# A hybrid attention block in Strassen-Winograd pairs: gate functions moved into the first products, two loads moved a pair ahead, buffers shared out anew

## The chip, the cores and the metric

The kernel runs on one core of a Trainium2 chip. The core has a matrix engine (TensorE, PE; its weight loads are shown as PEld), a vector engine (VectorE, DVE), a scalar engine for functions (ScalarE, ACT), a general engine (GpSimd, POOL) and an engine that issues most of the transfers (SyncE, SP). Each works through its own queue in order. The metric is the device time of one launch in microseconds; lower is better.

## The reference

One layer of a decoder block on x of 1024 positions by 1024 channels, all in fp32. The input is normalised, one projection gives all parts, two token mixers run beside each other (retention, differential attention), each is normalised per head and multiplied by SiLU of its gate, projected, multiplied by a sigmoid gate, and the sum goes through the output projection.

```python
h = rms_norm(x, norm_g)
z = einsum('bsd,dn->bsn', h, w_in)
(q_r, k_r, v_r, gate_r, q_d, k_d, v_d, gate_d, mg_r, mg_d) = split(z, ...)
o_r = rms_norm(retention(q_r, k_r, v_r), ret_norm_g) * silu(gate_r)
y_r = einsum('bse,ed->bsd', o_r, ret_w_o)
o_d = rms_norm(diff_attention(rms_norm(q_d), rms_norm(k_d), v_d, lam), sub_g) * 0.8
o_d = o_d * silu(gate_d)
y_d = einsum('bse,ed->bsd', o_d, diff_w_o)
m = sigmoid(mg_r) * y_r + sigmoid(mg_d) * y_d
x = x + einsum('bsd,de->bse', m, w_out)
```

## The kernel before

Each fp32 operand is split into a high and a low part, and a product is three matmuls (high x high, high x low, low x high; lines 101 and 126 to 133). The program runs in these stages.

1. The input is normalised and transposed; projections and retention follow, then eight heads of the differential attention. Work that is due later is handed to a clock (`after`, `tick`, `drain`) and mixed among the matmuls of the next products (`among`).
2. The gates: four projections of 1024 columns (two for SiLU, two for sigmoid), cut into 16 pairs of 2 x 128 columns: q = 0 to 7 are SiLU pairs, 8 to 15 sigmoid pairs. Each pair is one Strassen-Winograd step of 2 x 2 blocks with seven products. Two of the seven are made early, in `first_duo`, where both pairs of a duo use the two PSUM banks of the tag `pj`: the first half (kh 0) gives the product P1, the second (kh 1) adds P2 to it, which is the finished block C11. Both are copied out of PSUM (line 232 on ACT, line 234 on DVE) through tiles `ft` of the tag `gt` (three buffers) and stored to `first_d` in DRAM. Duos 0 and 2 run at the end of retention, 4 to 10 at the end of the attention, with its last heads still in the mix, and 12 and 14 after that.
3. The gate stage, `rests(pairs)`: for each pair the five products that are left, in `one` and `two` of the class `Pair`. A pair's `first` loads P1 (`p1_h`, shown as `p_h` in the profile) and copies it into the bank `y` (line 899), to which products are added; ACT copies `y` out between them (`u2`, `u3`, line 843: `u_h`), and the next product must wait for that copy. DVE subtracts `u` from the bank `z` (`c_h`, line 837), ACT applies the function (lines 914, 918), in the SiLU pairs DVE multiplies by the mixer's output `o` (line 915), and SP stores the result to `og` or `sg`. One pair ahead, `prep` loads the pair's weights (`ra_h`, `rb_h`), makes their sums and splits (`s_h`, `ls_h`, `l_h`), and then (line 925 on) loads C11 back into `c_first`, applies the function on ACT, multiplies and stores it.
4. The two projections of the mixers (`y0`, `y1`: first products, then pairs again, with gates `s` and sums `m` loaded as `ld` tiles), and the output projection (`out`) with x loaded as `ld` tiles.

Right operands of the gate stage: `t_h` are sums of quarters of the transposed input, loaded on POOL's queue and split on ACT and DVE (lines 690, 691); `hT` are the quarters that are still there.

Buffers of the later stages, each 128 x 512 fp32: results `c` come from the tag `gt` (three), `p1` has two, `u2` and `u3` two each, and `ld` (o, s, m, x) four. Those but `gt` lie in a pool that is opened when the attention's pool is closed. Instructions are put in order within each engine's queue when the program is built, and buffers turn round in a ring: an instruction that writes into a buffer waits for the last use of what was in it.

Of the kernel before, what the change touches and what calls it, by code (L numbers as in the profile page):

```python
# [9 lines left out]
F32 = mybir.dt.float32  # L10
# [52 lines left out]
def tile_hybrid_block(ctx, tc, x, norm_g, w_in, ret_norm_g, ret_w_o, dq_g, dk_g,  # L63
# [160 lines left out]
    def first_duo(q, following):  # L224

        banks = [pst("pj", f"fb{q + i}") for i in range(2)]
        for kh in range(2):
            among(sum([product(banks[i], F[q + i][kh], hq[kh, 0], kh == 0) for i in range(2)], []))
            for i in range(2):
                t = gp.tile([P, 512], F32, tag="gt", name=f"ft{q + i}{kh}", bufs=3)  # L230
                if kh == 0:
                    nc.scalar.activation(t, banks[i], AF.Copy)  # L232
                else:
                    nc.vector.tensor_copy(t, banks[i])
                nc.sync.dma_start(first_d[q + i][:, kh, :], t)
            if kh == 0:
                following()
            tick()
# [585 lines left out]
    class Pair:  # L824
# [15 lines left out]
        def u(self, tag):  # L840

            t = temp(tag, f"{tag}_{self.name}", 2)
            nc.scalar.activation(t, self.y, AF.Copy)  # L843
            return t
# [47 lines left out]
    def gate_pair(q):  # L892
        br, gate = q // 4 % 2, q < 8

        def first():
            p1 = temp("p1", f"p1_h{q}", 2)
            nc.sync.dma_start(p1, first_d[q][:, 0, :])
            y = bank(f"y_h{q}", "g")
            nc.scalar.activation(y, p1, AF.Copy)
            return y  # L900

        def pre(strip, half):
            if gate:
                h = 2 * (q % 4) + strip
                o = temp("ld", f"o{br}{h}{half}", 4)
# [3 lines left out]
        def done(strip, half, src, t, o):  # L909
# [3 lines left out]
            if gate:  # L913
                nc.scalar.activation(t, src, AF.Silu)
# [9 lines left out]
        def prep_and_c11():  # L924
            prep()
            t = temp("c", f"c_first{q}")
            nc.sync.dma_start(t, first_d[q][:, 1, :])
            done(0, 0, t, t, pre(0, 0))
# [27 lines left out]
    for br, wo in enumerate((ret_w_o, diff_w_o)):  # L956
        def calls(p, br=br):
            whole_sum = br == 1 and p == 3

            def pre(strip, half):  # L960
                i = 2 * p + strip
                o = [temp("ld", f"s{br}{i}{half}", 4)]
                nc.sync.dma_start(o[0], rows(sg[br][i], half))
                if whole_sum:
                    o.append(temp("ld", f"m{i}{half}", 4))
# [33 lines left out]
    def calls_out(i):  # L999
# [4 lines left out]
        def pre(strip, half):  # L1004
            xt = temp("ld", f"xr{i}{strip}{half}", 4)
# [40 lines left out]
```

## Time and profile before

| | us |
|---|---|
| median of 3 runs (1316.33 to 1317.63) | 1316.62 |
| the profiled execution, whole | 1319.1 |
| its span | 1317.3 |
| TensorE busy | 1263.8 |
| granted clock, mean | 0.991 |

All times in the text are microseconds from the start of the profiled span. A row of the timeline has start, length, engine, line, operation, output<-input, count, and in brackets the idle time ahead of it with what ended it. Buffer numbers are left out in the names: `c_h<-z_h,u_h` stands for all pairs. A row of `SPq` or POOL with DMA_DIRECT2D is the issue of a transfer. In the waits, "A <- B" says that A's engine stood idle until B was done.

### The profile page before, as it was taken

To read this page: it belongs to the slowest core of one execution; us is meant where nothing else is said; L and a number is where in the kernel's file an instruction comes from. 1 tells how busy PE (TensorE), PEld (TensorE's weight loads), DVE (VectorE), ACT (ScalarE), POOL (GpSimd) and SP (SyncE) were. 2 spreads that over 40 slices of the span, in tenths; PEclk is the share of its full clock that TensorE was granted. 3 is DMA by queue.
4 is the path that set the end of the run, shared out by engine and by line. 5 is a ranking of instruction groups with operands and counts; after the bars stand their busy time and mean duration, and the time that the engine had idled before them with its cause. 6 is when DMAs were issued, how large, how long until landed. Compare 5 with 4: busy or idle time off the path is not lost.

```text
span 1317.3 us, 19920 instructions
## 1 busy us (share of the span) xinstructions
PE 1263.8 (96%) x6836; PEld 1112.6 (84%) x6836; DVE 903.9 (69%) x1928; ACT 683.6 (52%) x1522; POOL 288.2 (22%) x403
## 2 busy tenths in 40 slices
PE   7998999999999999999999998998889999999798
PEld 5877888889999999999999886887778887877587
DVE  6777534745777868787787854865546688886583
ACT  6233213526676757667676743644554664443440
POOL 3133203323433425343332302000000000014100
PEclk9999999999999999999999999999899999999899
DMA  7375320240120201021020347887655887878873
GB/s 258 97 234 174 96 80 8 79 155 8 42 60 7 65 9 57 10 57 52 15 81 9 112 148 276 281 271 239 205 198 194 260 285 248 290 241 222 242 223 116
DMA packets 165173, 187.78 MB, mean 143 GB/s; under 512 B 10944, under 2 KB 109392, under 8 KB 165072
## 3 DMA queue, kind: packets, MB, share of 16 engines
q1 hardware_dynamic: 159936, 173.12, 40.7%
q0 software_dynamic: 5136, 13.39, 4.1%
q8 instruction: 54, 0.88, 0.3%
q14 instruction: 47, 0.39, 0.1%
HBM read 131.94 MB, written 54.53 MB: 142 GB/s over the span
## 4 chain that ended last, share of the span: by engine, by line
PE 66%; DMA 13%; issue 11%; DVE 5%; ACT 2%; POOL 2%; SPq 1%; DVEq 0%; POOLq 0%; ACTq 0%
PE z_d L121 20%; PE y_h L130 6%; PE fb L130 5%; PE sps L563 5%; PE dops L603 5%; PE z_rqk L121 5%; PE z_rv L121 4%; PE z_h L130 4%; PE y_out L130 2%; PE aT L590 2%; DMA og<-cb 2%; DMA c_first<-first 2%; DMA or_wr<-in_w_out_dram 2%; PE z_out L130 2%; DMA md<-cb 2%
## 5 line engine op out<-in xcount | busy, mean ns | idle before, releaser
L121 PE MATMUL z_d<-w_d,hT 128*128 128x384 f32 x1536 | 300.6, 340 | 0.6 <-DVE nsq L518 0.6
L121 PEld LDWEIGHTS z_d<-w_d,hT 128*128 128x128 f32 x1536 | 264.1, 188 | 2.8 <-DVE nsq L518 0.9
L569 ACT ACTIVATE S<-S,ast 128x256 f32<-128x256 f32 (+7 forms) x128 | 98.7, 772 | 29.3 <-DVE ast L565 27.9
L563 PE MATMUL sps<-K,Q 128*128 128x512 f32 (+5 forms) x384 | 107.8, 364 | 0.3 <-ACT Q L544 0.3
L130 PE MATMUL y_h<-t_h,ls_h 128*128 128x512 f32 x384 | 96.9, 403 | 11.3 <-ACT u_h L843 11.3
L130 PE MATMUL fb<-hT,fw 128*128 128x512 f32 x384 | 96.6, 402 | 7.5 <-ACT ft L232 7.1
L130 PEld LDWEIGHTS y_h<-t_h,ls_h 128*128 128x128 f32 x384 | 73.9, 194 | 29.5 <-ACT u_h L843 14.0
L121 PE MATMUL z_rv<-w_rv,hT 128*128 128x512 f32 x384 | 98.7, 397 | 0.0
L121 PE MATMUL z_rqk<-w_rqk,hT 128*128 128x512 f32 x384 | 95.9, 403 | 1.5 <-ACT hT L284 1.5
L130 PEld LDWEIGHTS fb<-hT,fw 128*128 128x128 f32 x384 | 71.6, 192 | 22.5 <-ACT ft L232 7.8
L121 PEld LDWEIGHTS z_rqk<-w_rqk,hT 128*128 128x128 f32 x384 | 72.0, 193 | 16.5 <-ACT hT L284 2.1
L603 PE MATMUL dops<-V,aTs 128*128 128x128 f32 x576 | 81.7, 275 | 0.0
L603 PEld LDWEIGHTS dops<-V,aTs 128*128 128x128 f32 x576 | 78.5, 191 | 2.6
L980 POOL DMA_DIRECT2D md<-cb x6 | 5.6, 933 | 337.9 <-DVE cb L973 337.9
L121 PEld LDWEIGHTS z_rv<-w_rv,hT 128*128 128x128 f32 x384 | 68.8, 188 | 11.8
L565 DVE CUSTOM_DVE_ANT_0 S<-sps,ndist 128x512 f32<-128x512 f32 (+5 forms) x128 | 67.6, 535 | 5.1 <-PE sps L563 4.6
L91 POOL TENSOR_TENSOR nss<-ms_n,mh 128x4 f32<-128x4 f32 x64 | 65.9, 1029 | 4.1
L520 POOL TENSOR_TENSOR nsq<-nsq,gh 128x256 f32<-128x256 f32 x64 | 50.1, 787 | 73.4 <-DVE nsq L518 61.8
L563 PEld LDWEIGHTS sps<-K,Q 128*128 128x128 f32 x384 | 63.3, 190 | 2.3 <-ACT Q L544 0.9
L580 DVE SCALAR_TENSOR_TENSOR S<-S,ast,S 128x128 f32<-128x128 f32 (+3 forms) x64 | 56.6, 884 | 1.3
L130 PE MATMUL y_y<-t_o,ls_y 128*128 128x512 f32 x192 | 47.9, 393 | 5.1 <-ACT ls_y L690 4.2
L90 POOL TENSOR_SCALAR ms_n<-nss 128x4 f32<-128x4 f32 x64 | 18.2, 285 | 154.6 <-DVE nss L514 151.9
(226 smaller groups left out, 2672.2 us busy)
## 6 DMA issues: line engine op xcount, KB each, us to landing
wr_d<-in_w_in_dram SPq DMA_DIRECT2D x96, 128.0 KB, 2.6
fr<-in_w_in_dram SPq DMA_DIRECT2D x16, 512.0 KB, 4.3
first<-ft SPq DMA_DIRECT2D x32, 256.0 KB, 2.5
ra_h<-in_w_in_dram SPq DMA_DIRECT2D x16, 512.0 KB, 4.2
rb_h<-in_w_in_dram SPq DMA_DIRECT2D x16, 512.0 KB, 4.7
s<-sg SPq DMA_DIRECT2D x32, 256.0 KB, 5.3
xt<-in_x_dram SPq DMA_DIRECT2D x8, 512.0 KB, 7.9
wr_rqk<-in_w_in_dram SPq DMA_DIRECT2D x16, 256.0 KB, 5.7
```

The lines of the kernel that those rows point to most:

```text
L90: nc.gpsimd.tensor_scalar(ms, ss, m, EPS, ALU.mult, ALU.add)
L91: nc.gpsimd.tensor_tensor(out_t, ms, mh[:, :n], ALU.pow)
L121: nc.tensor.matmul(o, a[k][:, i0, asl], b[k][:, i1, bsl], start=(k == 0 and j == 0), stop=(k == NK - 1 and j == 2))
L130: nc.tensor.matmul(bank, L[:, i0, j * P:(j + 1) * P], R[:, j, i1, :], start=(start and j == 0 and i == 0), stop=(j == 3 and i == 2), skip_ ...
L520: nc.gpsimd.tensor_tensor(sq, sq, hd["g"], ALU.mult)
L563: nc.tensor.matmul(sp[:, :m], hd["Q"][t][:, j, e, :], hd["K"][:, j, c], start=(e == 0), stop=(e == 1))
L565: nc.vector.tensor_tensor_reduce(sb[:, c], sp[:, :m], ndist[:, S - n + m * f:S - n + m * f + m], -slope, FMAX if f == 0 else st[:, j:j + 1 ...
L569: nc.scalar.activation(sb[:, :n], sb[:, :n], AF.Exp, bias=st[:, j:j + 1], scale=-1.0, accum_out=st[:, 2 + j:3 + j])
L580: nc.vector.scalar_tensor_tensor(S0[:, :n], S1[:, :n], st[:, 6:7], S0[:, :n], ALU.mult, ALU.add)
L590: nc.tensor.transpose(tp[:, b * P:(b + 1) * P], A[:, c:c + P], ident)
L603: nc.tensor.matmul(o[:, :P], aT[:, b, :], hd["V"][f][:, b, :], start=(kb == 0), stop=(kb == t))
L980: nc.gpsimd.dma_start(m, t, accum_op=ALU.add)
```

## The change

- In `first_duo` both halves are copied out by ACT. The second half gets the gate's function at once: Silu for q below 8, Sigmoid from 8 on. For the sigmoid pairs the finished block goes straight to its place in `sg`, and is not loaded again. Duos 12 and 14 take their tiles from `ld` instead of `gt`.
- In the gate stage P1 is loaded in `prep`, one pair ahead, into an `ld` tile. C11 is loaded in the SiLU pairs alone; it needs no function any more, only the multiply by `o`.
- Result tiles `c`: every fourth comes from a tile of its own, so four for three. `ld` has six buffers for four; `p1` has none of its own, `u3` one for two.

```diff
+    GATE = {0: AF.Silu, 1: AF.Sigmoid}
+
+    def first_duo(q, following, room=None):
...
-                t = gp.tile([P, 512], F32, tag="gt", name=f"ft{q + i}{kh}", bufs=3)
-                if kh == 0:
-                    nc.scalar.activation(t, banks[i], AF.Copy)
-                else:
-                    nc.vector.tensor_copy(t, banks[i])
-                nc.sync.dma_start(first_d[q + i][:, kh, :], t)
+                t = (room(f"ft{q + i}{kh}") if room else
+                     gp.tile([P, 512], F32, tag="gt", name=f"ft{q + i}{kh}", bufs=3))
+                nc.scalar.activation(t, banks[i], GATE[q // 8] if kh else AF.Copy)
+                dst = first_d[q + i][:, kh, :]
+                if kh and q >= 8:
+                    dst = sg[(q - 8) // 4][2 * ((q + i) % 4)][:, 0:512]
+                nc.sync.dma_start(dst, t)
...
     def temp(tag, name, bufs=None):
         if tag == "c":
-            return gp.tile([P, 512], F32, tag="gt", name=name, bufs=3)
+            turn["c"] = turn.get("c", 0) + 1
+            if turn["c"] % 4:
+                return gp.tile([P, 512], F32, tag="gt", name=name, bufs=3)
+            bufs = 1
...
-            t = temp(tag, f"{tag}_{self.name}", 2)
+            t = temp(tag, f"{tag}_{self.name}", 2 if tag == "u2" else 1)
...
+        p1 = []
+
         def first():
-            p1 = temp("p1", f"p1_h{q}", 2)
-            nc.sync.dma_start(p1, first_d[q][:, 0, :])
             y = bank(f"y_h{q}", "g")
-            nc.scalar.activation(y, p1, AF.Copy)
+            nc.scalar.activation(y, p1[0], AF.Copy)
             return y
...
-                o = temp("ld", f"o{br}{h}{half}", 4)
+                o = temp("ld", f"o{br}{h}{half}", 6)
...
             if gate:
-                nc.scalar.activation(t, src, AF.Silu)
+                if src is not None:
+                    nc.scalar.activation(t, src, AF.Silu)
                 nc.vector.tensor_tensor(t, t, o, ALU.mult)
...
         def prep_and_c11():
+            p1.append(temp("ld", f"p1_h{q}", 6))
+            nc.sync.dma_start(p1[0], first_d[q][:, 0, :])
             prep()
-            t = temp("c", f"c_first{q}")
-            nc.sync.dma_start(t, first_d[q][:, 1, :])
-            done(0, 0, t, t, pre(0, 0))
+            if gate:
+                t = temp("c", f"c_first{q}")
+                nc.sync.dma_start(t, first_d[q][:, 1, :])
+                done(0, 0, None, t, pre(0, 0))
...
-    first_duo(12, lambda: more(14, 15))
+    def room(name):
+        return temp("ld", name, 6)
+
+    first_duo(12, lambda: more(14, 15), room)
...
-    first_duo(14, pairs[0].prep)
+    first_duo(14, pairs[0].prep, room)
```

The loads of `s`, `m` and `xr` in the projections ask for six buffers in the same way.

The change also moves instructions in the queues. The names below carry the number of the pair (`c_first6` is C11 of pair 6; `ft121` is the tile of pair 12, second half), and a counter at the end that is without meaning here.

**The last duos, SP's queue**, where the last output of the attention (`ot_d7<-doT71`) is stored. Before:

```order
L235 DMA first11_121<-ft111_9126 128x512
L643 DMA ot_d7_87<-doT71_9108 128x512
L906 DMA o000_9295<-ot_r0_78 128x512
L235 DMA first12_122<-ft120_9165 128x512
L897 DMA p1_h0_9381<-first0_110 128x512
L906 DMA o011_9386<-ot_r0_78 128x512
L906 DMA o020_9429<-ot_r0_78 128x512
L766 DMA rb_h1_9401<-in_w_in_dram 128x4x256
L906 DMA o010_9467<-ot_r0_78 128x512
L897 DMA p1_h1_9471<-first1_111 128x512
L235 DMA first13_123<-ft130_9168 128x512
L765 DMA ra_h2_9490<-in_w_in_dram 128x4x256
```

After, at the same place:

```order
L238 DMA sg04_96<-ft101_9123 128x512
L937 DMA c_first0_9295<-first0_110 128x512
L937 DMA c_first1_9428<-first1_111 128x512
L238 DMA sg06_98<-ft111_9126 128x512
L646 DMA ot_d7_87<-doT71_9108 128x512
L937 DMA c_first2_9517<-first2_112 128x512
L238 DMA first12_122<-ft120_9165 128x512
L238 DMA first13_123<-ft130_9168 128x512
L769 DMA rb_h1_9402<-in_w_in_dram 128x4x256
L238 DMA sg10_100<-ft121_9211 128x512
L768 DMA ra_h2_9490<-in_w_in_dram 128x4x256
L238 DMA sg12_102<-ft131_9214 128x512
```

Four loads of `o` and two of P1 that stood between the stores of duo 12 have moved behind them; three loads of C11 stand ahead instead, two of them ahead of the attention's last store.

**A SiLU pair, ACT's queue** (`c_h…` is the Silu of a result, `l22` a split, `u2` the copy of the bank). Before:

```order
L914 ACTIVATE c_h211_9703<-c_h211_9703 128x512
L914 ACTIVATE c_h101_9708<-c_h101_9708 128x512
L690 ACTIVATE l22_h4_9757<-rb_h4_9737 128x512
L843 ACTIVATE u2_h3_9770<-y_h3_9719 128x512
L914 ACTIVATE c_first4_9763<-c_first4_9763 128x512
L690 ACTIVATE ls4_h4_9760<-s4_h4_9743 128x512
L914 ACTIVATE cb210_9808<-y_h2_9596 128x512
```

After, and below it SP's queue in a SiLU pair of the changed kernel:

```order
L921 ACTIVATE c_h311_9823<-c_h311_9823 128x512
L921 ACTIVATE c_h201_9828<-c_h201_9828 128x512
L693 ACTIVATE l22_h5_9877<-rb_h5_9857 128x512
L849 ACTIVATE u2_h4_9889<-y_h4_9837 128x512
L693 ACTIVATE ls4_h5_9880<-s4_h5_9863 128x512
L921 ACTIVATE cb310_9927<-y_h3_9715 128x512
```

```order
L923 DMA og01_89<-c_h201_9828 128x512
L912 DMA o110_9955<-ot_d1_81 128x512
L769 DMA rb_h7_10101<-in_w_in_dram 128x4x256
L923 DMA og10_90<-c_first5_9883 128x512
L912 DMA o101_9957<-ot_d0_80 128x512
L937 DMA c_first6_10005<-first6_116 128x512
L912 DMA o131_9962<-ot_d3_83 128x512
L923 DMA og01_89<-cb310_9927 128x512
L933 DMA p1_h6_9976<-first6_116 128x512
L768 DMA ra_h8_10222<-in_w_in_dram 128x4x256
L923 DMA og10_90<-c_h411_9945 128x512
```

The activation of C11 is gone from ACT. On SP the load of `c_first6` waits for the store of `c_first5`, two rows ahead of it, since both use the same tile; P1 of pair 6 is loaded in the pair before.

**The end of the attention, ACT's queue** (`S` is the exponential of the scores, `fw` a weight split, `Q`, `aTs` and `fsq` copies and squares of the attention). Before:

```order
L232 ACTIVATE ft50_8716<-fb5_8620 128x512
L84 ACTIVATE fw100_8992<-fr10_8990 128x512
L592 COPY aTs740_8641<-aT740_8636 128x512
L544 ACTIVATE Q77_8708<-tq77_8703 128x2x128
L545 ACTIVATE Q77_8708<-tq77_8703 64x2x128
L546 ACTIVATE Q77_8708<-tq77_8703 64x2x128
L625 ACTIVATE fsq70_8661<-O70_8338 128x512
L569 ACTIVATE S751_8563,ast75_8530<-S751_8563,ast75_8530 128x768
```

After:

```order
L234 ACT_TABLE_LOAD
L234 ACTIVATE ft41_8810<-fb4_8619 128x512
L84 ACTIVATE fw100_8992<-fr10_8990 128x512
L595 COPY aTs740_8641<-aT740_8636 128x512
L547 ACTIVATE Q77_8708<-tq77_8703 128x2x128
L548 ACTIVATE Q77_8708<-tq77_8703 64x2x128
L549 ACTIVATE Q77_8708<-tq77_8703 64x2x128
L628 ACTIVATE fsq70_8661<-O70_8338 128x512
L572 ACT_TABLE_LOAD
L572 ACTIVATE S751_8563,ast75_8530<-S751_8563,ast75_8530 128x768
L234 ACT_TABLE_LOAD
L234 ACTIVATE ft51_8813<-fb5_8620 128x512
```

Each change between exponential and gate function brings a load of the function table: 14 in the whole program, where there were 9 (one at the start, eight in the gate stage).

More of the change, by code (lines that the diff above doesn't have):

```diff
@@ L1004, in pre @@
         def pre(strip, half):
-            xt = temp("ld", f"xr{i}{strip}{half}", 4)
+            xt = temp("ld", f"xr{i}{strip}{half}", 6)
             nc.sync.dma_start(xt, place(x, strip, half))
```

5 lines of the change are left out of this document (2 added, 3 removed).

## The prediction

> **What bounds the kernel now.** I read the page first, then busy times by stretch, then the order of instructions in time where TensorE (PE) is not full.
>
> ```profile
> span 1317.3 us, 19920 instructions
> PE 1263.8 (96%) x6836; PEld 1112.6 (84%) x6836; DVE 903.9 (69%) x1928; ACT 683.6 (52%) x1522; POOL 288.2 (22%) x403
> ```
>
> PE is the bound over the whole span, so only stretches in which it stands still or runs on a lower granted clock can be won. The change removes no matmul. The stretches:
>
> ```profile
> 770.00:830.00 60.00, 53.42 (x249) 44.09 (x248) 30.28 (x51) 23.05 (x42) 11.56 (x19) 0.94 0.66 221
> 880.00:970.00 90.00, 79.26 (x332) 63.41 (x330) 50.16 (x80) 44.27 (x72) 0.00 (x0) 0.96 0.68 220
> 970.00:1062.00 92.00, 91.41 (x396) 75.51 (x397) 57.25 (x89) 53.60 (x98) 0.00 (x0) 0.98 0.70 230
> 1200.00:1260.00 60.00, 51.22 (x214) 40.56 (x213) 35.85 (x58) 23.06 (x41) 13.97 (x21) 0.94 0.89 252
> ```
>
> Columns: stretch, length, busy PE, PEld, DVE, ACT, POOL, granted clock, DMA share, GB/s. PE loses time in the last two first-product duos (770 to 830), in the Silu pairs of the gate stage (880 to 970) and where the output projection begins (1200 to 1260); the sigmoid pairs (970 to 1062) are nearly full. How much the Silu pairs lose, from PE's own rows:
>
> ```profile
> 883.12 2.88 PE L130 MATMUL y_h<-t_h,l_h 128*128 128x512 f32 x12
> ...
> 918.57 3.02 PE L130 MATMUL y_h<-t_h,ls_h 128*128 128x512 f32 x12 [2.66 <-ACT u_h L843]
> ...
> 982.09 2.88 PE L130 MATMUL y_h<-t_h,l_h 128*128 128x512 f32 x12
> ...
> 995.69 2.88 PE L130 MATMUL y_h<-t_h,l_h 128*128 128x512 f32 x12
> ...
> 1036.49 2.88 PE L130 MATMUL y_h<-t_h,l_h 128*128 128x512 f32 x12
> ```
>
> The product with `l_h` comes once in each pair. From 995.69 to 1036.49 lie three pairs: 13.60 each, with no wait. From 883.12 to 982.09 lie six: 98.97, where 6 x 13.60 = 81.6 would do. **The Silu pairs lose 17.4 us**, waits and the slower matmuls behind them together. The reason stands on ACT:
>
> ```profile
> 911.77 0.63 ACT L914 ACTIVATE c_h<-c_h 128x512 f32<-128x512 f32 x1
> ...
> 913.78 0.32 SPq L927 DMA_DIRECT2D c_first<-first  x1
> ...
> 916.88 0.63 ACT L914 ACTIVATE c_first<-c_first 128x512 f32<-128x512 f32 x1 [4.48 <-DMA c_first<-first]
> 917.42 0.61 ACT L690 ACTIVATE l_h<-rb_h 128x512 fp32r<-128x512 f32 x1
> 917.94 0.58 ACT L843 ACTIVATE u_h<-y_h 128x512 f32<-128x512 f32 x1
> ```
>
> ACT stands at the activation of the reloaded C11 (`c_first`) until its load lands; behind it in the queue is `u_h`, the copy that PE needs before it may add to the bank again. PE's row at 918.57 is released by just that copy.
>
> **The change, part by part.**
>
> *Gate stage.* The activation of `c_first` leaves ACT's queue: 16 of them, 0.63 each, 10 us of ACT, and with it the wait. What is then late?
>
> ```profile
> PE y_h L130 <- ACT u_h L843: 7.5, 5, 3.2
> ACT c_first L914 <- DMA c_first<-first: 11.3, 6, 4.5
> DVE c_first L915 <- DMA o<-ot_d: 7.8, 4, 3.3
> ```
>
> (Total, times, longest, from 830 to 970.) DVE still multiplies `c_first` by `o` in the Silu pairs, and the order shows the `o` load of that multiply behind the same store as before. So DVE keeps waits like those of the last row, 1.95 in the mean, 3.3 at most. How much PE bears: without the c_first wait, in the pair whose last Silu begins at 911.77 and ends near 912.4, `l_h` and `u_h` would be done near 913.5, while PE had work up to 918.57 - 2.66 = 915.9; 2.4 of slack. The longest wait exceeds that by 1, the mean doesn't; I charge 0.4 for each of six pairs, 2.4. **Term A: -17.4 + 2.4 = -15.0**, bounds 0 (the wait moves whole) and -17.4. In the sigmoid pairs c_first disappears altogether, with 8 loads, 8 stores and 8 activations; PE waited little there, so I take nothing. `u3` with one buffer is read by DVE a pair before it is written again: nothing.
>
> *Last duos.* The two stalls of the duos at their end:
>
> ```profile
> 797.76 13.87 PE L130 MATMUL fb<-hT,fw 128*128 128x512 f32 x60
> 811.96 3.01 PE L130 MATMUL fb<-hT,fw 128*128 128x512 f32 x12 [0.33 <-DVE ft L234]
> 821.22 7.61 PE L130 MATMUL fb<-hT,fw 128*128 128x512 f32 x24 [6.24 <-ACT ft L232]
> 828.66 1.52 PE L130 MATMUL z_h<-t_h,ls_h 128*128 128x512 f32 x6
> ```
>
> ```profile
> 808.04 0.63 ACT L690 ACTIVATE t_h<-t_h 128x512 fp32r<-128x512 f32 x1 [2.65 <-DMA t_h<-h_t]
> ...
> 809.80 13.74 SPq L235 DMA_DIRECT2D first<-ft  x4
> ...
> 811.85 0.63 ACT L690 ACTIVATE t_h<-t_h 128x512 fp32r<-128x512 f32 x1 [0.37 <-DMA t_h<-h_t]
> ...
> 820.57 0.60 ACT L232 ACTIVATE ft<-fb 128x512 f32<-128x512 f32 x1 [8.08 <-DMA first<-ft]
> ```
>
> ACT waits 8.08 for one of three `gt` tiles to be stored, and PE for ACT. At 13.60/60 = 0.227 a matmul the 96 matmuls from 797.76 would end at 819.5; they end at 828.66: 9.1 lost, part of it to the clock (24 matmuls in 7.61 where 5.4 would do). With six `ld` tiles this wait goes. Next late are the `t_h` conversions that now stand ahead of the copies on ACT, and twelve of them are due before the pairs start: the first four ran at 808.04 to 811.85, 1.27 apart; the twelfth would be at 808.04 + 11 x 1.27 = 822.0, cut and subtracted at 823.3. **Term B: 823.3 - 828.66 = -5.4**, bounds 0 and -9.1.
>
> *Gate functions in the duos.* The copies on DVE (16 x 0.69) become ACT functions. On DVE that is off the path. On ACT they bring switches of the function table:
>
> ```profile
> 952.44 0.62 ACT L690 ACTIVATE ls_h<-s_h 128x512 fp32r<-128x512 f32 x1
> 953.08 1.28 ACT L914 ACT_TABLE_LOAD   x1
> 954.37 0.60 ACT L914 ACTIVATE cb<-y_h 128x512 f32<-128x512 f32 x1
> ```
>
> ```profile
> 745.00:755.00 10.00, 10.00 (x55) 8.61 (x54) 9.47 (x27) 7.49 (x19) 1.38 (x3) 1.00 0.45 149
> 755.00:765.00 10.00, 10.00 (x54) 8.60 (x54) 7.04 (x17) 5.53 (x11) 0.86 (x1) 1.00 0.43 131
> ```
>
> ```profile
> 756.23 0.37 ACT L609 ACTIVATE O<-dops,ast 128x128 f32<-128x128 f32 x1 [3.15 <-PE dops L603]
> ```
>
> A load is 1.28 and from 953.06 (the end before it) to 954.37 pass 1.31. The order has 14 loads for 9; seven of the new ones stand between Exp and Silu or Sigmoid at the end of the attention, with eight moved functions of 0.60: 7 x 1.28 + 8 x 0.60 = 13.8 us of ACT. Where they are densest, 745 to 765, ACT has 13.0 of 20 busy and gets four loads and two functions, 6.3: 19.3 of 20. It just fits. PE's next matmul behind each function has other work ahead of it in PE's order (12 matmuls of the other bank, scores, transposes), so I charge little: **term D: +1**, bounds 0 and +13.8. In the Silu to Sigmoid turn of the gate stage four loads fewer remain; that is in term A.
>
> The Trainium skill speaks against this part: in "ScalarE: Activation LUTs", What ACT_TABLE_LOAD costs, a switch is a load of 1283 ns and a drain of about 1380 ns, and the page's advice is to do all of one set before switching. The rows above show the load, but no drain beyond 0.03 us; by the page's price the seven switches and eight functions would be an estimated 7 x 2.66 + 4.8 = 23.4 of ACT instead of 13.8, and the forecast with all of it on PE's path 1317 instead of 1308. By the rows the trace does not agree with the drain.
>
> *Six load tiles, four result tiles in the projections.* At the start of the output projection:
>
> ```profile
> L130 PE MATMUL X_out<-r_w,la_out 128*128 128x512 f32 x96 | 24.8, 415 | 8.5 <-ACT la_out L690 7.7 <-ACT y_out L819 0.8
> ```
>
> ```profile
> 1229.03 5.09 DMA m<-md
> ```
>
> The load of `m`, a load tile that had to wait for its turn, is on the chain of waits; with six it is issued earlier. But PE's 8.5 us hang on stores to `md` and loads of `rf_out`, which stay. **Term C: -2**, bounds +1 and -8.5.
>
> **Sum:** -15.0 - 5.4 + 1 - 2 = -21.4. The profiled execution took 1319.1 (span 1317.3); the median of the runs is 1316.6. 1316.6 - 21.4 = **1295**.
>
> **Rivals.**
>
> *The wait goes from ACT to DVE.* For it: DVE waits in order as ACT did, and c_first's multiply has the splits and `c_h` of the pair behind it. If its `o` wait falls on PE in full, six pairs keep 6 x 1.95 = 11.7, and term A is -5.7: 1304. Against it: 2.4 of slack in each pair.
>
> *ACT becomes the bound of the attention's end.* For it: 19.3 of 20. If all 13.8 fall on PE: 1295 + 12.8 = 1308. Against it: ACT has gaps there like the 3.15 before 756.23, and PE other work.
>
> *More comes back.* Terms A, B at their bounds and C at -4: 1316.6 - 17.4 - 9.1 + 1 - 4 = 1287.
>
> *Slower: C11's own tile.* With four result tiles in a Silu pair every fourth is the new one, and it is always c_first; the order shows each c_first load behind the store of the c_first before it. That is a ring: multiply, store, load, multiply.
>
> ```profile
> c_first<-first SPq DMA_DIRECT2D x6, 256.0 KB, 3.3
> ...
> og<-c_first SPq DMA_DIRECT2D x3, 256.0 KB, 2.6
> ```
>
> ```profile
> first<-ft SPq DMA_DIRECT2D x9, 256.0 KB, 5.7
> ...
> o<-ot_r SPq DMA_DIRECT2D x4, 256.0 KB, 9.7
> ```
>
> By the first two rows (880 to 970) the ring takes 0.7 + 2.6 + 3.3 and two issues of 0.3: 7.2, under 13.6. By the last two (797 to 830, with the queues full) it takes 0.7 + 5.7 + 9.7 + 0.6 = 16.7, and eight pairs at 16.7 lose 24.8, 7.4 more than now; without terms B and C, which full queues would take too, and with +1, 1325. It decides from a ring of 13.6 + 17.4/8 = 15.8. Against it: the change takes 4 MB of transfers out and the pairs before 880 kept their pace.
>
> *Nothing moves.* The stores, not the tiles, are late, and the waits stay where they are under other names: 1316.6, with term D 1318.
>
> **How the numbers follow.** Forecast 1295 (1290 to 1300) 0.50; wait to DVE 0.18 (1300 to 1308); ACT the bound 0.09 (1302 to 1310); more comes back 0.10 (1284 to 1290); nothing moves 0.06; slower 0.07. The predicted time is that of the likeliest, 1295. The range 1287 to 1310 leaves out half of "more", all of "nothing" and "slower": 0.18. Of a measurement of this kernel 0.2%, 2.6 us, can be told from no change: faster 0.87, same 0.06, slower 0.07.
>
> **What would show it.** Term A: the `l_h` products of the Silu pairs 13.6 to 14.2 apart, and no ACT wait for c_first; if DVE waits over 3 us for c_first or `o` and PE behind it for ACT's `u_h`, the first rival holds, and if c_first's multiply waits for a load issued as its own last store lands, the ring. Term B: no ACT wait for first<-ft, and from the oT transpose ahead of the last duos to the first z_h matmul about 26 us instead of 31. Term C: PE's wait before X_out at 6 to 7. Term D: PE waits of under 1 us for ACT's `ft` before the last duos. The forecast is wrong if the Silu pairs stay above 14.5 us, if the 9 us at the duos move to `t_h`, or if a stage that the change does not touch has grown.

## The result, and the profile after

The changed kernel took 1303.59 us in the median of four runs (1295.44 to 1306.9), the kernel before 1316.98 (1316.33 to 1317.63): 0.9889 of it, 95% interval 0.9843 to 0.9935, **faster by 1.1%**. Four further runs (the first experiment) gave 1299.92 against 1318.3: 0.9865, interval 0.9848 to 0.9881. The forecast was 1295 with a range of 1287 to 1310; the time lies in the range, and the gain, 13.4 and 18.4 us in the two sets, is short of the forecast 21.4 in both.

The profiled execution of the first set is its slowest run (1306.9, span 1305.1). First the page's totals, then the same three stretches as before (columns as in the prediction):

```profile
span 1305.1 us, 19856 instructions
PE 1263.1 (97%) x6836; PEld 1113.3 (85%) x6836; DVE 892.8 (68%) x1912; ACT 688.7 (53%) x1527; POOL 286.4 (22%) x403
```

```profile
770.00:830.00 60.00, 56.94 (x265) 46.92 (x265) 28.74 (x50) 34.56 (x62) 11.10 (x19) 0.97 0.70 240
880.00:970.00 90.00, 85.97 (x370) 69.90 (x369) 55.29 (x89) 41.89 (x73) 0.00 (x0) 0.98 0.67 221
970.00:1062.00 92.00, 92.00 (x408) 76.20 (x407) 60.97 (x97) 51.19 (x93) 0.00 (x0) 1.00 0.69 223
```

PE's full time rose from 53.42 to 56.94 of 60 in the duos and from 79.26 to 85.97 of 90 in the Silu pairs. Neither is full. PE's rows there:

```profile
798.37 5.71 PE L130 MATMUL fb<-hT,fw 128*128 128x512 f32 x24
804.38 5.74 PE L130 MATMUL fb<-hT,fw 128*128 128x512 f32 x24 [0.31 <-ACT ft L234]
812.88 12.82 PE L130 MATMUL fb<-hT,fw 128*128 128x512 f32 x48 [2.75 <-ACT ft L234]
825.53 0.84 PE L130 MATMUL z_h<-t_h,ls_h 128*128 128x512 f32 x3
```

```profile
907.13 2.88 PE L130 MATMUL y_h<-t_h,l_h 128*128 128x512 f32 x12
920.79 2.88 PE L130 MATMUL y_h<-t_h,l_h 128*128 128x512 f32 x12
925.68 3.04 PE L130 MATMUL y_h<-t_h,ls_h 128*128 128x512 f32 x12 [1.10 <-ACT u_h L849]
935.81 2.88 PE L130 MATMUL y_h<-t_h,l_h 128*128 128x512 f32 x12
940.12 3.02 PE L130 MATMUL y_h<-t_h,ls_h 128*128 128x512 f32 x12 [0.52 <-ACT u_h L849]
950.23 2.88 PE L130 MATMUL y_h<-t_h,l_h 128*128 128x512 f32 x12
956.42 4.44 PE L130 MATMUL y_h<-t_h,ls_h 128*128 128x512 f32 x12 [2.41 <-ACT u_h L849]
968.12 2.88 PE L130 MATMUL y_h<-t_h,l_h 128*128 128x512 f32 x12
```

The wait of 6.24 in the duos is now 2.75 (with 48 matmuls in 12.82 behind it, where 10.9 would do). The first six intervals of `l_h` are 13.6 or 13.7, then come 15.0, 14.4 and 17.9: the stall begins three pairs later than before and is smaller, but it is there, and again PE waits for ACT's `u_h`.

Where the time went is best seen by stage, since two stages that the change hardly touches differ between executions of one program. From PE's rows of each profiled execution: the start up to the last `qkTp` transpose, the attention up to the last `oT` transpose, the duos and gate pairs up to the sixteenth `l_h` product, and the rest (projections and output) to the end. The runs of an experiment are compared with runs of the kernel before that were made beside them (medians 1316.8 to 1318.4), so kernels are best compared by the ratio; two ratios whose intervals overlap are not told apart.

| kernel | span | start | attention | duos + pairs | rest | median of runs, ratio to before (95%) |
|---|---|---|---|---|---|---|
| before | 1317.3 | 264.6 | 532.8 | 263.3 | 256.6 | |
| changed | 1305.1 | 265.0 | 533.1 | 248.8 | 258.3 | 1303.6, 0.9889 (0.9843–0.9935) |
| changed, again | 1297.1 | 261.9 | 532.2 | 248.1 | 254.9 | 1299.9, 0.9865 (0.9848–0.9881) |
| gate functions alone | 1303.0 | 263.4 | 532.4 | 253.9 | 253.3 | 1305.5, 0.9907 (0.9891–0.9923) |
| tiles and early loads alone | 1314.5 | 261.6 | 532.6 | 261.7 | 258.6 | 1316.3, 0.9988 (0.9973–1.0004) |
| last duos on three tiles | 1297.9 | 262.3 | 532.5 | 248.8 | 254.3 | 1301.0, 0.9874 (0.9856–0.9892) |
| ra, rb on POOL's queue | 1300.3 | 263.6 | 532.3 | 245.7 | 258.7 | 1300.0, 0.9867 (0.9850–0.9883) |
| the same, duos on three tiles | 1302.7 | 264.3 | 531.8 | 252.5 | 254.1 | 1308.2, 0.9938 (0.9919–0.9956) |
| Silu for sigmoid in the pairs | 1296.2 | 262.9 | 532.3 | 245.2 | 255.8 | 1298.1, 0.9852 (0.9840–0.9865) |
| c_first on POOL's queue | 1304.6 | 263.6 | 531.9 | 253.8 | 255.2 | 1302.5, 0.9885 (0.9863–0.9908) |
| four load tiles | 1306.1 | 264.9 | 532.0 | 252.8 | 256.5 | 1307.6, 0.9929 (0.9908–0.9950) |
| four, and a tile for ra | 1306.0 | 264.2 | 532.3 | 251.4 | 258.1 | 1303.1, 0.9891 (0.9866–0.9917) |
| the same, on POOL's queue | 1299.4 | 264.3 | 532.0 | 251.6 | 251.5 | 1305.4, 0.9906 (0.9876–0.9936) |
| no ring | 1301.7 | 263.3 | 532.5 | 243.5 | 262.4 | 1303.4, 0.9885 (0.9866–0.9904) |

The gain of the change is in the fourth column: 263.3 to 248.8 and 248.1, 14.6 and 15.2 us. The attention took the same time in all fourteen within 1.3. The start differs by 3.4, though its program is the same in all of them, and the rest by 11.

### The profile page after: what moved, and what is told of

Read it like the earlier page. It is cut to its first block, busy times and chain, and to the rows that moved or that the text cites. A ratio compares the mean times of both kernels' runs of the same rounds, so it can differ in the third digit from the quotient of the medians.

```text
span 1305.1 us, 19856 instructions
## 1 busy us (share of the span) xinstructions
PE 1263.1 (97%) x6836; PEld 1113.3 (85%) x6836; DVE 892.8 (68%) x1912; ACT 688.7 (53%) x1527; POOL 286.4 (22%) x403
## 4 chain that ended last, share of the span: by engine, by line
PE 63%; issue 13%; DMA 10%; DVE 8%; ACT 3%; POOL 2%; SPq 1%; DVEq 0%; POOLq 0%; ACTq 0%
PE z_d L121 19%; PE y_h L130 6%; PE fb L130 5%; PE sps L566 5%; PE z_rqk L121 5%; PE dops L606 5%; PE z_rv L121 4%; PE z_h L130 4%; PE aT L593 2%; PE y_out L130 2%; DMA rb_h<-in_w_in_dram 2%; DMA or_wr<-in_w_out_dram 2%; PE z_out L130 1%; PE tq L543 1%; DMA rb_out<-md 1%
## 5 line engine op out<-in xcount | busy, mean ns | idle before, releaser
L130 PE MATMUL y_h<-t_h,ls_h 128*128 128x512 f32 x384 | 94.0, 395 | 4.0 <-ACT u_h L849 4.0
L121 PEld LDWEIGHTS z_rqk<-w_rqk,hT 128*128 128x128 f32 x384 | 71.8, 192 | 16.3 <-ACT hT L287 2.0
```

The source lines that it names most:

```text
L121: nc.tensor.matmul(o, a[k][:, i0, asl], b[k][:, i1, bsl], start=(k == 0 and j == 0), stop=(k == NK - 1 and j == 2))
L130: nc.tensor.matmul(bank, L[:, i0, j * P:(j + 1) * P], R[:, j, i1, :], start=(start and j == 0 and i == 0), stop=(j == 3 and i == 2), skip_ ...
```

## The experiments

Three theories stood at the outset. The changed kernel's missing gain is (1) a wait that DVE took over from ACT, the prediction's rival; (2) a ring of its own in the gate stage; (3) the function tables.

**Changed kernel again.** No edit.

> The changed kernel once more, in five rounds. Its four times so far lie 11.5 us apart (1295.4 to 1306.9), those of the kernel before 1.3. Theory: the spread is one stage in which a stall hangs on when DMA transfers land, the Silu pairs of the gate stage; then a profile that is some us shorter has its Silu pairs nearer to 13.6 apart, the rest the same to 1 us. Rival: the spread is the granted clock (0.992 in the first profile), then all stages shrink alike.

1299.92 (1298.92 to 1301.12). The profile is 8.0 us shorter than the first one: 3.1 in the start, 0.8 in the attention, 0.6 in duos and pairs, 3.4 in the rest. So **both theories on the spread are wrong**: the Silu pairs are nearly the same in both (196.1 and 197.0 from the first to the fifteenth `l_h`), and the stages don't shrink alike. What differs is in the last section. It also says how to read the rest: single profiles are compared here in the stage that an edit touches, and the runs' medians beside them.

**Gate functions alone; tiles and early loads alone.** The changed kernel split in two. The first is the kernel before with

```diff
-                if kh == 0:
-                    nc.scalar.activation(t, banks[i], AF.Copy)
-                else:
-                    nc.vector.tensor_copy(t, banks[i])
+                nc.scalar.activation(t, banks[i], GATE[q // 8] if kh else AF.Copy)
```

and C11's activation taken out of the pairs; the second is the changed kernel with these lines turned back.

> The kernel before with the gate functions alone: Silu or sigmoid in the duos, no activation of c_first, the sigmoid pairs' C11 stored as a result at once; tiles and loads as before (three result tiles, four load tiles, p1 loaded at its use, duo copies on gt). Theory, by the prediction's terms: most of term A and term D, no term B: 1317 - 10.8 (what the gate stage gained in the first profile) + 0.6 = 1306 to 1307. Rival, that the tiles and the early loads carry the gain of the gate stage: 1313 to 1318, with the Silu pairs as in the kernel before.

> The changed kernel without the gate functions: C11's activation is again in the pairs (with its wait on ACT), the duos' copies alternate between ACT and DVE, all eight sigmoid pairs load their C11 again; tiles and early loads as changed. Theory: the wait of ACT on c_first is back, its load is only issued one pair ahead as before, so the gate stage keeps its 17 us of loss, and only the duos' 3.8 remain: 1313 (1310 to 1316). Rival, tiles and early loads carry the gain: 1300 to 1308.

1305.48 and 1316.29. The gate functions alone bring 12.8 us, the tiles alone 2.0 (their interval holds no change), both together 18.4: the tiles are worth more once the gate functions have moved. The second kernel lies just above the 1310 to 1316 expected: it gained in the duos (24.8 from the last `oT` transpose to the first `z_h` product, 31.3 before) and lost half of that in the pairs (211.2 from the first to the fifteenth `l_h`, 207.8 before). The old wait is back in it; its waits between 825 and 985 (total, times, longest):

```profile
ACT c_first L918 <- DMA c_first<-first: 17.0, 5, 8.1
```

In the first kernel it is gone, and DVE waits for `o`, as the rival had it (first row):

```profile
922.77 0.69 DVE L918 TENSOR_TENSOR c_first<-c_first,o 128x512 f32<-128x512 f32 x1 [7.72 <-DMA o<-ot_d]
...
924.22 0.69 DVE L700 TENSOR_TENSOR s_h<-ra_h,rb_h 128x512 f32<-128x512 f32 x1 [0.15 <-DMA rb_h<-in_w_in_dram]
```

The two intervals of `l_h` around it are 15.4 and 16.4. The wait of the first rival is there, with the old four load tiles; but the `s_h` behind it waits a further 0.15 for `rb`, so it isn't shown that `o` alone held DVE. With six load tiles DVE waits 4.7 for `o` at most, and behind that, in the second profile of the changed kernel, 1.37 more for `rb`:

```profile
911.61 0.69 DVE L922 TENSOR_TENSOR c_first<-c_first,o 128x512 f32<-128x512 f32 x1 [4.69 <-DMA o<-ot_d]
...
914.28 0.69 DVE L701 TENSOR_TENSOR s_h<-ra_h,rb_h 128x512 f32<-128x512 f32 x1 [1.37 <-DMA rb_h<-in_w_in_dram]
```

There `rb` lands last, not `o`.

**The last two duos on the three gt tiles.**

```diff
-    first_duo(12, lambda: more(14, 15), room)
+    first_duo(12, lambda: more(14, 15))
...
-    first_duo(14, pairs[0].prep, room)
+    first_duo(14, pairs[0].prep)
```

> The changed kernel, the last two duos' copies again on the three gt tiles instead of the load tiles. Theory: the duos lose their 3.8 us again and the gate stage is as in the changed kernel: 3 to 5 above it, about 1307, with ACT's wait on the store first<-ft back at 6 to 8 us. Rival, that the wait only moves (load tiles held by the duos make the first pairs' p1 and o loads late): the same time as the changed kernel within 1.5, or less.

1300.98, 1.1 above the changed kernel: the rival's number. Its reason isn't seen, since in the changed kernel the first six intervals are 13.6 and no first pair is late; the duos lost what the theory expected; ACT's wait is back, and PE's behind it:

```profile
818.07 0.60 ACT L234 ACTIVATE ft<-fb 128x512 f32<-128x512 f32 x1 [8.01 <-DMA first<-ft]
```

```profile
818.72 8.37 PE L130 MATMUL fb<-hT,fw 128*128 128x512 f32 x24 [6.25 <-ACT ft L234]
```

From the last `oT` transpose to the first `l_h` product pass 45.7 instead of 41.4. But then the pairs take 192.4 from the first to the fifteenth `l_h` instead of 196.1: the first eight intervals are 13.6 and the turn's is 15.6. **What the load tiles win in the duos, the pairs lose again.** Something other than PE sets when the Silu pairs end. The second profile of the changed kernel shows it (rows of SP, DVE, ACT in order of time):

```profile
922.75 0.43 SPq L769 DMA_DIRECT2D rb_h<-in_w_in_dram  x1
```

```profile
928.33 0.69 DVE L701 TENSOR_TENSOR s_h<-ra_h,rb_h 128x512 f32<-128x512 f32 x1 [5.30 <-DMA rb_h<-in_w_in_dram]
...
932.20 0.68 DVE L843 TENSOR_TENSOR c_h<-z_h,u_h 128x512 f32<-128x512 f32 x1
```

```profile
932.92 0.63 ACT L921 ACTIVATE c_h<-c_h 128x512 f32<-128x512 f32 x1 [7.00 <-DVE c_h L843]
...
934.65 0.62 ACT L693 ACTIVATE l_h<-rb_h 128x512 fp32r<-128x512 f32 x1
935.18 0.58 ACT L849 ACTIVATE u_h<-y_h 128x512 f32<-128x512 f32 x1
```

```profile
935.81 0.68 DVE L694 TENSOR_TENSOR l_h<-rb_h,l_h 128x512 fp32r<-128x512 f32 x1
```

```profile
936.80 0.45 SPq L769 DMA_DIRECT2D rb_h<-in_w_in_dram  x1
```

A ring: `rb` lands, DVE goes on with `s_h` and, behind it in its order, `c_h`; then ACT's Silu, behind that `l_h` and `u_h` (for which PE waits); DVE's `l_h`, and 0.3 us behind its end the next `rb` load. One round is 14.05 here, 15.5 and 15.6 the ones before and after it; PE needs 13.60.

**Is it SP's order or the tile that holds rb back?** The loads of `ra` and `rb` on POOL's queue, in the changed kernel and in the one with the duos on three tiles:

```diff
-        nc.sync.dma_start(ra, src(0, 0, 2))
-        nc.sync.dma_start(rb, src(1, 0, 2))
+        queue = nc.gpsimd if name[0] == "h" else nc.sync
+        queue.dma_start(ra, src(0, 0, 2))
+        queue.dma_start(rb, src(1, 0, 2))
```

> The changed kernel with the loads of the gate pairs' ra and rb on POOL's queue instead of SP's; POOL does nothing else in that stage. Theory: what is left of the gate stage's loss is a ring of its own, slower than PE: DVE ends l_h, only then SP, which stood behind the stores of c_h, issues the rb load of the next pair (922.43 to 922.75 in the second profile of the changed kernel), 5.6 to landing, DVE's s_h rows and c_h 10 us behind it, ACT, l_h: 14.1 to 15.6 a round where PE needs 13.60. The buffer that rb takes (ra of the pair before) has been free for 6 us by then. On POOL's queue rb is issued those 4 to 6 us earlier and DVE's waits for rb_h (23 us between 825 and 965) all but go: Silu pairs 13.6 apart but for the turn to sigmoid, 3 to 6 less than the changed kernel, 1294 to 1297. Rival: rb waits for its buffer, not for SP: then it is issued at l_h's end as before, same time within 1.5. Second rival: POOL's issues are slow, or its queue is held by a wait of ra: up to 5 more.

> The same edit (ra and rb on POOL's queue) in the kernel whose last duos copy to the three gt tiles again. Theory of the ring: the ring, not PE, set the end of the Silu pairs, so the 4.3 us that the load tiles gained in the duos (41.4 instead of 45.7 from the last oT transpose to the first l_h product) were lost again in the pairs (196.1 instead of 192.4). With the ring gone this kernel gains only 0 to 2 on its own 1301, and stands 3.5 to 4.5 above the run with load tiles in the duos, where without the edit it stood 1.1 above. Rival, the duos' gain is lost for another reason (load tiles held by the duos): the two stay within 1.5 of each other.

1300.04 (0.9867), the same as the changed kernel: **the first rival holds**. Duos and pairs are 2.4 us shorter in its profile (245.7), where 3 to 6 were expected, and DVE's waits for `rb_h` stay (23.7 us between 795 and 965). POOL's rows name what the loads wait for:

```profile
921.67 0.75 POOL L770 DMA_DIRECT2D rb_h<-in_w_in_dram  x1 [4.05 <-DVE l_h L694]
930.88 0.75 POOL L769 DMA_DIRECT2D ra_h<-in_w_in_dram  x1 [8.46 <-DVE s_h L701]
936.42 0.75 POOL L770 DMA_DIRECT2D rb_h<-in_w_in_dram  x1 [4.79 <-DVE l_h L694]
```

`rb` stands at the head of a queue that only `ra` shares here, and still starts 0.3 us behind the end of an `l_h`. In the built program that is the `l_h` of the pair two back, which reads the tile last: the expectation's sentence that the tile had long been free was wrong. The second kernel is a miss and tells nothing of the ring: at 1308.2 it is 7 to 8 us above the same kernel without the edit. The conversions of `t_h`, whose loads share POOL's queue, came late (DVE waited 17.0 us for ACT's, 11.3 at once), the first `z_h` product 35.3 us after the last `oT` transpose instead of 32.1.

**The turn from Silu to sigmoid.**

```diff
-                nc.scalar.activation(t, src, AF.Sigmoid)
+                nc.scalar.activation(t, src, AF.Silu)
```

> The changed kernel with Silu in place of sigmoid in the second eight pairs' activations (not in the duos): part of the gates is then another function. It takes the three table loads of the turn (1.28 each) away. Theory: two of the three stand in the ring of the turn's pair (before the Silu c_h at 948.83 and before cb at 952.29), the first lies in a wait; the longest interval of l_h products, 17.65, falls to about 15, the others stay: 1.3 to 2.6 less than the changed kernel, 1297.5 to 1298.6. Rival, the turn's interval is long because of the sigmoid pair's own loads: no change within 1.5.

1298.08, 1.8 under the changed kernel (0.9852 against 0.9865 of the kernel before; the intervals overlap, so the stage has to show it). The rows:

```profile
931.95 2.88 PE L130 MATMUL y_h<-t_h,l_h 128*128 128x512 f32 x12
946.71 2.88 PE L130 MATMUL y_h<-t_h,l_h 128*128 128x512 f32 x12
961.75 2.88 PE L130 MATMUL y_h<-t_h,l_h 128*128 128x512 f32 x12
975.35 2.88 PE L130 MATMUL y_h<-t_h,l_h 128*128 128x512 f32 x12
```

The longest interval falls from 17.65 to 15.0, and from the first to the fifteenth product pass 193.2 instead of 196.1 (the changed kernel's two profiles differ by 0.9 there): the loads at the turn cost 2.9 there, near the 2.6 of the two that stand in the ring. The Trainium skill, "ScalarE: Activation LUTs", What ACT_TABLE_LOAD costs, adds a drain of about 1380 ns to each switch; two of them would be an estimated 5.3 us. The 2.9 agree with the loads alone.

**c_first on POOL's queue.**

```diff
-                nc.sync.dma_start(t, first_d[q][:, 1, :])
+                nc.gpsimd.dma_start(t, first_d[q][:, 1, :])
```

> The changed kernel with the loads of c_first on POOL's queue. Theory on the duos: the store of the last attention output stood on SP behind two c_first loads that wait for the duos' sg stores, so the last two duos' ft waits of 4.3 and 2.75 on ACT and PE start there; without them the stretch from the last oT transpose to the first l_h product falls by 1 to 3 from 41.4. By the ring theory that gain is lost again before the sigmoid pairs, and the whole is within 1.5 of the changed kernel. Rival, the gain stays: 1 to 3 less.

1302.5, 2.6 above the changed kernel, which neither expectation had, though the intervals overlap; in the duos a part of the theory is seen:

```profile
808.53 11.17 PE L130 MATMUL fb<-hT,fw 128*128 128x512 f32 x48 [1.48 <-ACT ft L234]
819.54 2.20 PE L130 MATMUL z_h<-t_h,ls_h 128*128 128x512 f32 x9
825.97 5.20 PE L130 MATMUL y_h<-t_h,ls_h 128*128 128x512 f32 x12 [4.23 <-ACT y_h L905]
```

The attention's last store is issued only 0.4 earlier than in the changed kernel, but ACT's wait for it falls from 4.38 to 2.69; whether that is the order or the traffic of the `c_first` loads wasn't separated. The `t_h` loads, which wait for that store, begin 4.5 us after the last `oT` transpose instead of 6.6; PE's wait for the copy is 1.48, the 48 matmuls behind it take 11.17, and the first `z_h` product comes 24.0 us after that transpose instead of 27.8. Then PE waits 4.23 for `y_h`, whose `p1` was late, and the gain is gone before the first `l_h` (44.3, where the theory asked for 1 to 3 less than 41.4). So a part of the stall left in the duos came with the two loads ahead of that store; the rival, that the gain stays, is wrong. They are not its only cause: two kernels that leave them there reach the first `z_h` as early, tiles alone after 24.8 and `ra`, `rb` on POOL's queue after 24.9.

**One raw tile more.** The ring theory says that a free tile breaks it. Four load tiles for six are the control (first line, and so at each `ld`); their 4 KB then go to a tile for `ra`, which leaves the three raw tiles to `rb`:

```diff
-                o = temp("ld", f"o{br}{h}{half}", 6)
+                o = temp("ld", f"o{br}{h}{half}", 4)
...
-        r = wpool.tile([P, 2, 512], F32, tag="wraw", name=name, bufs=3)
+        r = (fp.tile([P, 2, 512], F32, tag="ra", name=name, bufs=1) if name[1] == "a" else
+             wpool.tile([P, 2, 512], F32, tag="wraw", name=name, bufs=3))
```

> The changed kernel with four load tiles instead of six, everything else as changed (the last two duos still copy to them). Control for the next kernel. Theory: the two further load tiles are worth 0 to 3; in the pairs the ring of the rb loads decides, not the tiles: 1300 to 1303, Silu pairs again with intervals of 14 to 18 behind the sixth. Rival, the load tiles carry the gain over the kernel with the gate functions alone (5.5 us): 1304 to 1306.

> Four load tiles, and the 4 KB that this frees used for a tile of ra's own, so that the three raw tiles are left to rb. On POOL's queue rb was issued 0.3 us behind DVE's end of l_h as it was on SP's, so it is its tile that rb waits for: that of the rb two pairs before, which l_h reads last. With three of them rb waits for the l_h three pairs before. Theory of the ring (rb's landing, DVE's s_h, c_h behind it in DVE's order, ACT, l_h, next rb): it is broken, DVE's waits for rb_h (23 us between 825 and 965) fall below 6 us, the Silu pairs are 13.6 apart but for the turn (15 to 16), 192 to 193 from the first to the 15th l_h product instead of 196 to 197; 3.5 to 5 less than ld4. Rival, the o loads or ACT's order set these intervals: same as ld4 within 1.5.

> The same with ra and rb of the gate pairs on POOL's queue. Theory: with a tile free a pair earlier, rb's place in SP's order (behind stores that wait for c_h) counts; on POOL's queue it is issued as soon as its tile is free: 0 to 2 less than raw4. Rival, ra, which has one tile, holds POOL's queue until DVE's s_h of the pair before, and rb behind it: the ring comes back in another form, 1 to 4 more than raw4.

The control is 1307.61: the theory of its expectation is wrong, the two load tiles are worth some 8 us by the runs, 4 to 5 of them in duos and pairs by the profiles. Its ACT waited 33 us for `p1`, which shares the load tiles. With ra's tile 1303.11, 4.5 less than the control, as the ring theory asked (the intervals still overlap a little), and DVE's waits for `rb_h` are gone. From the first to the fifteenth `l_h` pass 196.8 us, 201.0 in the control, where the theory asked for 192 to 193: the first interval is 16.3 and the third to sixth are 14.1 to 15.0, and DVE now waits for `ra_h` (17.9 us, 13.4 of them once). From the eighth on all intervals are 13.6, the turn's among them, with its table loads in place. On POOL's queue 1305.4, with wide runs (1297.5 to 1308.7) that tell nothing against either. Its profile, though, has what no other had; the two windows hold ten pairs, the turn among them:

```profile
855.00:940.00 85.00, 85.00 (x376) 70.38 (x375) 63.23 (x103) 39.78 (x72) 10.49 (x14) 1.00 0.85 282
940.00:1000.00 60.00, 60.00 (x266) 49.69 (x265) 34.51 (x54) 31.15 (x52) 5.99 (x8) 1.00 0.51 172
```

PE is full at the full clock: 13.6 for every pair, though the table loads are all there, and though DVE in these windows still waits 4.1 us for `o` once and 4.4 for a store. **With the ring broken neither the tables nor the waits of DVE cost PE anything there.** What it lost lies ahead of that: ra's new tile lies where the attention's tiles lay, so the first `ra` was issued 8.4 us behind the last `oT` transpose, where the changed kernel issues it 17.4 ahead; DVE's first `s_h` came 10 us later behind that transpose than in the changed kernel, and the second group of `t_h` loads at 14.8 instead of 10.2 us.

**No ring, with the start mended.** First pair's `ra` in a raw tile, the POOL queue from pair 4 on, paid with one load tile (five) and one stage tile (six).

```diff
+        r = (fp.tile([P, 2, 512], F32, tag="ra", name=name, bufs=1)
+             if name[1] == "a" and name != "ra_h0" else
...
-        return lpool.tile([P, 512], F32, tag="rs", name=name, bufs=7)
+        return lpool.tile([P, 512], F32, tag="rs", name=name, bufs=6)
...
+        queue = nc.gpsimd if name[0] == "h" and int(name[1:]) >= 4 else nc.sync
```

> The changed kernel with a tile of its own for ra from the second gate pair on (the three raw tiles then serve rb), paid for with one load tile (five for six) and one stage tile (six for seven), and with the ra and rb loads of pairs 4 to 15 on POOL's queue; the first pair's ra stays in a raw tile, since a new tile can only be loaded when the attention's tiles are free, which in the run with all ra in the new tile made ra and the t_h loads late. Theory: with the rb ring gone the pairs run 13.6 apart through the turn as they did there, and with the start as in the changed kernel the stretch from the last oT transpose to the last l_h product falls from 248 to 242 to 244: 4 to 6 less than the changed kernel, 1294 to 1298. Rival, fewer load and stage tiles or the later ra of the second pair cost the same again at the start of the stage: 1299 to 1306, with the loss before the third l_h product.

The stage does what the theory said: 243.5 from the last `oT` transpose to the last `l_h` product (242 to 244 expected, 248.1 without the edit), and all intervals behind the second product are 13.6, the turn's among them. The time doesn't: 1303.44, within the rival's numbers, but hardly for its reason, since the third product comes only 1.1 later than in the changed kernel. The rest takes 262.4 instead of 254.9, of which 4.1 is more than the changed kernel's own two profiles (254.9 and 258.3) differ by. The loss is in the projections. The two stretches, this kernel first, then the second profile of the changed kernel:

```profile
1058.00:1078.00 20.00, 15.92 (x64) 12.18 (x63) 17.04 (x29) 10.51 (x20) 0.00 (x0) 0.94 0.71 237
...
1138.00:1168.00 30.00, 25.10 (x103) 20.02 (x103) 25.34 (x43) 13.76 (x25) 3.48 (x4) 0.94 0.77 225
```

```profile
1060.00:1080.00 20.00, 18.19 (x79) 14.32 (x78) 17.94 (x31) 10.88 (x21) 0.00 (x0) 1.00 0.73 239
...
1140.00:1170.00 30.00, 28.07 (x122) 22.45 (x122) 28.10 (x47) 14.32 (x26) 6.51 (x9) 1.00 0.83 235
```

PE waits longer for the splits of the projections' weights (`ls_y`: 4.2 in one wait, 1.3 at most in the other kernel) and loses clock behind it. The kernel with four load tiles and ra's single tile on POOL's queue, which serves the projections too, took only 251.5 in the rest, with 1.2 as its longest wait for `ls_y`. So a missing load tile and ra's single tile don't make this loss by themselves; the missing stage tile, or loads that start no earlier though PE does, are left, and weren't tried apart. No version that computes the same block is shown to be faster than the changed kernel.

## Why the prediction was right, and where its sizes were off

The mechanism was right: the wait of ACT on `c_first` was the main loss, it is gone, and the kernel is faster by more than the runs differ. The sum was 5 to 6 us too large in duos and pairs by the stage table (20.4 forecast, 14.6 and 15.2 measured), and that lies in the sizes of terms:

- **Term A, forecast -15.0, measured -10.8 and -11.7** (207.8 to 197.0 and 196.1 from the first to the fifteenth `l_h`). The step that failed is "the longest wait exceeds that by 1, the mean doesn't; I charge 0.4 for each of six pairs, 2.4". It looked for the next late thing in the `o` load of `c_first`'s multiply and weighed it by one pair's slack. What is left, 6.6 and 5.7, is the ring of the `rb` loads, whose round of 14 to 15.6 exceeds 13.60 by little and adds up over the pairs: some 2.9 are the table loads in its turn, 2.8 the rest of it (193.2 - 190.4 in the run without these loads). The term also took the interval of the turn from 19.4 to 13.6, though three table loads stay there (at 944, 953 and 957 in the first profile); it measured 17.9 and 17.7, so 4.3 and 4.1 of what is left lie in that one interval.
- **Term B, forecast -5.4, measured -3.7 and -3.5** (from the last `oT` transpose to the first `z_h`: 31.3 to 27.5 and 27.8). The wait for first<-ft went as said, though ACT then waits 4.3 and 4.4 for the attention's last store instead; the step that put the `t_h` conversions next was right on what is late, but it took their start from the kernel before (10.6 us after the transpose; 12.0 and 11.7 measured): the store of the attention's last output, for which their loads wait, had moved behind two `c_first` loads on SP, and the 2.75 that PE waited cost 1.9 of clock as well. With those loads elsewhere it was 24.0; it was also under 25 in two kernels with the loads where they are, so the rest of the cause stays open.
- What neither term saw: A and B are not independent. The duos' gain of 4.3 is 0.7 or nothing at the end of the pairs (248.1 and 248.8 against 248.8), which the ring would explain, if its rounds are set by the loads and not by when PE starts. That stays argued, since the kernel meant to test it was a miss.
- **Term D, forecast +1, measured 0.2 and -0.6** (532.8 to 533.1 and 532.2). Seven switches and eight functions on ACT cost the attention's tail nothing that can be seen; the rival "ACT the bound" is wrong.
- **Term C, forecast -2, measured +1.8 and -1.7**: within what this stage does by itself.
- **The rivals.** "The wait goes from ACT to DVE" gave 1304, and the first set's 1303.6 is nearer to it than to 1295; that is luck. By the prediction's own sign (DVE over 3 us for `o`, and PE behind it for `u_h`) it would hold, but in the second profile `rb` landed later than `o` behind the longest of these waits, and in a kernel without the ring DVE still waits 4.1 for `o` while PE is full. "Slower" and "nothing moves" were wrong: no wait for `c_first`'s own tile shows among the changed kernel's waits from 825 to 985, and the tiles alone gain 2.0 with an interval that holds no change.

## What to carry to other kernels

A stall that has been removed can uncover a ring, and not the next single wait: follow one buffer from its load round to the next load of the same buffer, over every in-order engine between, and compare that round with the engine that is the bound; here half a microsecond in a round was lost in full. A gain ahead of such a ring wasn't kept here, so the gains of two neighbouring stages need not add. And tiles and queues that one stage gives up can be what the next stage lived on, so an edit has to be read in the stages behind it too.

## What the runs showed of the hardware that was not expected

**What a wait of PE of about 2 us costs differs between executions.** The same wait in the start of the two profiles of the changed kernel, first the wait, then the 4 us behind it:

```profile
109.71 0.49 PE L433 MATMUL ro<-v,sT 128*128 128x128 f32 x2 [2.37 <-DVE sT L425]
```

```profile
109.71:113.71 4.00, 4.00 (x23) 3.90 (x24) 2.16 (x4) 1.02 (x3) 0.56 (x1) 0.68 0.85 282
```

```profile
107.67 0.49 PE L433 MATMUL ro<-v,sT 128*128 128x128 f32 x2 [2.06 <-DVE sT L425]
```

```profile
107.67:111.67 4.00, 4.00 (x31) 3.87 (x32) 2.58 (x5) 1.54 (x3) 1.64 (x3) 1.00 0.88 296
```

After 2.37 the granted clock is 0.68 and 23 matmuls run in 4 us; after 2.06 it is 1.00 and 31 do. The length alone doesn't decide: at this same instruction the clock fell to 0.62 after a wait of 2.19 (`ra`, `rb` on POOL's queue) and stayed at 1.00 after 2.50 (gate functions alone); it fell in six of the fourteen profiles, whose waits there are 1.78 to 2.64. Over all fourteen profiles, of the waits of PE of at least 1 us behind the first 60 us, the mean clock of the next 4 us was under 0.8 in 4 of 42 waits shorter than 1.8 us, in 20 of 43 from 1.8 to 2.75, and in 32 of 34 longer ones. The kernel has waits near 2 us in every execution, in the start and, in most, in the duos, the turn and at the output's beginning, and a drop costs 1 to 2 us (8 matmuls of 31 here, 1.9 us behind the 2.75 in the duos). That can make up only part of the 8 us between these two profiles and of the spread of the runs: of the 3.1 in the start, 2.0 lie ahead of this wait already. How much it is wasn't measured. The Trainium skill, "TensorE: Matmul & The Clock Gate", HAM oscillation — how this bites in real kernels, warns of idle gaps above some 3.4 us; here shorter ones, from 1.8 us, already brought the drop about every second time. The Trainium skill, the same page, What's actually happening, says that the window in which PE's work is watched runs free, which agrees with a drop that comes in one execution and not in the next.

**A move of loads to another queue moved more than those loads.** From the last `oT` transpose to the first `z_h` product the kernels with `ra` and `rb`, with `c_first`, and with `ra`'s new tile on POOL's queue took 24.9, 24.0 and 32.9 us (30.1 with that tile on SP's queue), where the changed kernel takes 27.8: what else stood on the two queues, `t_h` on POOL's and the last store and `p1` on SP's, landed earlier or later with them.
